# A conditioning vector spread by products with ones, one norm's scaling on another engine, and new planner numbers in a two-network kernel

## The chip, the core and the metric

The kernel runs on one core of a Trainium2 chip. The core has a matrix engine (TensorE, PE in the profile), a vector engine (VectorE, DVE), an activation engine (ScalarE, ACT), a general one (GpSimd, POOL) and a queue engine that issues transfers here (SyncE, SP). The engines run side by side and wait for each other through semaphores. The metric is the device time of one execution in microseconds; a kernel's time is the median of its runs.

## The reference, cut to what matters

512 tokens of width 1024 pass two networks one after the other, in float32. The first has a convolution layer and an attention layer with forget gates, each followed by a gated feed-forward layer and by layer norms; every layer is modulated by a vector that is computed from `c`. The second mixes latent attention and a gated linear attention (HGRN2), followed by a feed-forward layer and a gated projection of `p`.

```python
c_act = jax.nn.silu(c)
for l in range(DEPTH):
    sh1, sc1, g1, sh2, sc2, g2 = jnp.split(c_act @ w_ada[l] + b_ada[l], N_MOD, axis=-1)
    h = modulate(x, sh1, sc1)
    y = short_conv_mixer(...) if l < N_A else forgetting_attention(...)
    x = layer_norm(DEEPNORM_ALPHA * x + g1[:, None, :] * y, ln1_g[l], ln1_b[l])
    h = modulate(x, sh2, sc2)
    y = swiglu(h, ffn_w_gate[l], ffn_w_up[l], ffn_w_down[l])
    x = layer_norm(DEEPNORM_ALPHA * x + g2[:, None, :] * y, ln2_g[l], ln2_b[l])
...
h = rms_norm(x, g_mix)
c_q, c_kv, k_r, hq, hf_f, hf_b, hi, hg = jnp.split(h @ w_in, IN_SPLITS, axis=-1)
x = x + jnp.concatenate([mla(c_q, c_kv, k_r, ...), hgrn2(hq, hf_f, hf_b, hi, hg, ...)], axis=-1) @ w_o
x = x + (silu(rms_norm(x, g_ffn) @ w_gate) * (rms_norm(x, g_ffn) @ w_up)) @ w_down
out = x + sigmoid(rms_norm(x, g_ple) @ w_ple_gate) * (p @ w_ple_proj)
```

## The kernel before

Activations lie transposed: 8 tiles of 128 features by 512 tokens. Each float32 operand of a weight product is split into a high and a low part of a shorter format, and one product is three matmuls: high by high, low by high, high by low. The names say which: `h_0h` and `h_0l` are the parts of the convolution's input tile 0, `whi` and `wlo` those of a pack of eight 128 by 128 weight blocks. A pack arrives as one transfer of 512 KB (`raw`), ACT casts it to `whi`, and DVE, or at some places POOL, subtracts to get `wlo`.

The stages follow the reference. `setup` (L957) loads `vec` (all small vectors), computes `pple` (the projection of `p`, tiles `pT`, which needs nothing else) and spreads `c` over 128 partitions as `cact`; the modulation vectors `ada` are products of rows of `w_ada` with `cact`, summed along the row on DVE. `conv_block` multiplies by three matrices (`gb`, `gc`, `vv`). `fox_block` is the forgetting attention: `pq`, `pk`, `pv` are its projections, `q0a`, `q0b`, `qz` its queries, written on 64 partitions, and `S` its scores. `ffn_ln` with `mix_ln` (L1530) is the second feed-forward layer and the layer norm behind it, done in two halves of 256 tokens; `axr` is the stream, `hx` its scaled split for the next network, and `cq` the first products there. `rope_tables` (L1494) builds sine and cosine from `posi`. In `block2` the latent attention has `MS`, `MP`, `mtp` (scores, probabilities, their transposes), and the tiles `gl`, `gs` belong to the linear attention.

All instructions are first recorded (so nearly all have one line in the profile, L603), then ordered by `plan()` and issued. `plan()` is a list scheduler: it walks in time over the five engines and gives each the ready instruction with the lowest number, by durations from `cost()` (L317) and a table of latencies. The number is the place in the program, less a shift of the instruction's group, a stage or a piece of one: `op.prio = op.i - op.shift - OFFSETS.get(op.group, 0)`. A DVE `tensor_tensor` without PSUM operands may go to POOL when DVE's queue is long; the planner counts that a DVE instruction with two SBUF operands, or a copy or scaling within SBUF, and a POOL `tensor_tensor` do not run side by side. The order inside an engine is then fixed; on the chip an engine waits at an instruction until its operands are there. SP issues all transfers in a fixed order too, on eight semaphores in turn, so each waits for the landing of the eighth before it.

## Time and profile before

| | us |
|---|---|
| median of 3 runs (lowest, highest) | 1895.33 (1893.64, 1896.21) |
| the profiled execution | 1893.86 |
| its span | 1892.2 |
| PE busy | 1868.3 |
| DVE busy | 1216.5 |
| ACT busy | 857.5 |
| POOL busy | 204.7 |
| mean granted clock of PE | 0.998 of full |

The span is the time from the first to the last recorded instruction; the execution's own time has a little around it. PE is almost never idle, so the views that count are those that show where it is, or where it runs slower: the table by windows, the list of what PE waited for, and the timeline around those places. An idle stretch of another engine costs nothing unless PE waits at its end.

### The profile page before, as it was taken

Reading aid. Unit: us, or ns where it says so; the run is one execution under the profiler, and the core shown is the slowest. Engines: PE = TensorE matmul, PEld = TensorE weight load, DVE = VectorE, ACT = ScalarE, POOL = GpSimd, SP = SyncE. Lnnn points to the kernel's source line nnn. Section 1 sums busy time; section 2 is a strip of 40 time slices with the busy share of each in tenths; the row PEclk is TensorE's granted clock in tenths of the full one; section 3 lists DMA queues with packets and bytes.
Section 4 is the critical chain, followed back from the end, with each engine's and each line's share of the span. In section 5 each row is a group of like instructions: output and inputs, shape, how many; then the busy total and the mean of one; then the engine's idle time right before and its main releaser. Section 6 shows DMA issues by size and latency. Waiting matters only on the chain.

```text
span 1892.2 us, 24315 instructions
## 1 busy us (share of the span) xinstructions
PE 1868.3 (99%) x9314; PEld 1572.5 (83%) x9314; DVE 1216.5 (64%) x2000; ACT 857.5 (45%) x1425; POOL 204.7 (11%) x204
## 2 busy tenths in 40 slices
PE   9999999999999999999999999999999999999998
PEld 7888888888888888898888888888887888888887
DVE  8887866567468876885333225998998645344455
ACT  5322722223339876663222223687886423122333
POOL 3101100000010210101000001023343000000000
PEclk9999999999999999999999999999999999999999
DMA  9675377467433113223232222322021322222331
GB/s 353 229 249 190 110 236 239 172 222 243 158 129 108 70 68 122 86 72 106 89 112 100 90 79 105 129 90 79 33 78 45 112 97 92 100 95 95 112 143 69
DMA packets 74325, 241.51 MB, mean 128 GB/s; under 512 B 8320, under 2 KB 9600, under 8 KB 74208
## 3 DMA queue, kind: packets, MB, share of 16 engines
q1 hardware_dynamic: 74208, 239.95, 36.6%
q8 instruction: 73, 1.20, 0.2%
q14 instruction: 44, 0.36, 0.1%
HBM read 231.46 MB, written 8.45 MB: 127 GB/s over the span
## 4 chain that ended last, share of the span: by engine, by line
PE 89%; DVE 6%; ACT 3%; issue 1%; DMA 1%; SPq 0%; DVEq 0%; ACTq 0%
PE pg L603 18%; PE pu L603 18%; PE pd L603 13%; PE gt L603 5%; PE ffn_down L603 5%; PE pv L603 2%; PE gb L603 2%; PE gc L603 2%; PE vv L603 2%; PE pk L603 2%; PE pl L603 2%; PE wo L603 2%; PE pq L603 2%; PE cq L603 2%; PE attn_o L603 1%; PE conv_out L603 1%
## 5 line engine op out<-in xcount | busy, mean ns | idle before, releaser
L603 ACT CAST whi<-raw 128x1024 fp32r<-128x1024 f32 (+1 forms) x313 | 325.4, 1043 | 616.2 <-PE pu L603 126.9
L603 DVE TENSOR_TENSOR wlo<-raw,whi 128x1024 fp32r<-128x1024 f32 (+1 forms) x287 | 354.4, 1238 | 337.0 <-ACT whi L603 321.5
L603 POOL TENSOR_TENSOR wlo<-raw,whi 128x1024 fp32r<-128x1024 f32 x26 | 67.6, 2602 | 1114.9 <-ACT whi L603 952.9
L603 DVE CUSTOM_DVE_ANT_0 aj<-ada,cact,adab 128x1024 bf16<-128x1024 f32 x96 | 126.3, 1318 | 32.5 <-DMA ada<-in_wada 32.0
L603 DVE TENSOR_TENSOR s<-pu,s 128x512 f32<-128x512 f32 x44 | 30.1, 687 | 46.5 <-PE pu L603 46.2
L603 ACT ACTIVATE s<-s 128x512 f32<-128x512 f32 x22 | 13.9, 632 | 77.1 <-DVE s L603 77.1
L603 ACT ACTIVATE s<-pg 128x512 f32<-128x512 f32 x44 | 26.0, 594 | 49.1 <-PE pg L603 49.1
L603 DVE TENSOR_TENSOR s<-pg,rfr 128x512 f32<-128x512 f32 x22 | 15.2, 690 | 40.4 <-PE pg L603 40.2
L603 DVE TENSOR_TENSOR S<-S,sq 128x512 f32<-128x512 f32 (+1 forms) x61 | 34.6, 567 | 0.4
L603 DVE CUSTOM_DVE_ANT_0 G<-S,cmask 128x128 f32<-128x128 f32 (+3 forms) x64 | 28.4, 487 | 4.2 <-PE S L603 3.4
L603 DVE TENSOR_TENSOR u<-pu,rfr 128x512 f32<-128x512 f32 x22 | 15.2, 690 | 23.4 <-PE pu L603 23.4
L603 DVE TENSOR_TENSOR xr<-pd,xr 128x512 f32<-128x512 f32 x16 | 11.0, 689 | 23.0 <-PE pd L603 23.0
L603 ACT ACTIVATE sq<-axr 128x256 f32<-128x256 f32 (+1 forms) x33 | 15.2, 467 | 21.1 <-DVE axr L603 21.1
L603 POOL MEMSET kz<- 32x512 f32 x32 | 16.8, 524 | 50.2 <-PE pd L603 14.7
L603 ACT ACTIVATE Pa<-G,negm 128x128 f32<-128x128 f32 (+1 forms) x32 | 16.2, 508 | 9.8 <-DVE negm L603 4.8
L603 PE MATMUL pg<-hm0l,whi 128*128 128x512 f32 (+1 forms) x48 | 18.0, 376 | 1.2 <-DVE hm0l L603 1.2
L603 PE MATMUL S<-kz,qz 128*128 128x256 f32 (+2 forms) x64 | 19.1, 329 | 0.0
L603 PE MATMUL pg<-hm3l,whi 128*128 128x512 f32 (+1 forms) x48 | 17.9, 373 | 1.0 <-DVE hm3l L603 1.0
L603 PE MATMUL pg<-hm6h,whi 128*128 128x512 f32 (+1 forms) x48 | 17.9, 373 | 0.8 <-ACT whi L603 0.8
L603 PE MATMUL pg<-hm0h,whi 128*128 128x512 f32 (+1 forms) x48 | 18.0, 376 | 0.6 <-ACT hm0h L603 0.6
L603 POOL MEMSET qz<- 32x512 f32 x32 | 17.0, 531 | 14.2 <-DVE ada L603 8.8
L603 PE MATMUL pg<-hm0h,wlo 128*128 128x512 f32 (+1 forms) x48 | 18.0, 374 | 0.5 <-DVE wlo L603 0.5
(3641 smaller groups left out, 6246.1 us busy)
## 6 DMA issues: line engine op xcount, KB each, us to landing
raw<-in_wpack SPq DMA_DIRECT2D x309, 512.0 KB
ada<-in_wada SPq DMA_DIRECT2D x96, 512.0 KB
ada<-in_wada SPq DMA_DIRECT2D x32, 256.0 KB
x<-in_xT SPq DMA_DIRECT2D x8, 256.0 KB
pd<-pple SPq DMA_DIRECT2D x8, 256.0 KB
xd<-x SPq DMA_DIRECT2D x8, 256.0 KB
axr<-xd SPq DMA_DIRECT2D x8, 256.0 KB
xd<-axr SPq DMA_DIRECT2D x8, 256.0 KB
```

Of the source, the lines that this page charges most:

```text
L603: getattr(getattr(nc, op.unit), op.name)(*[get(x) for x in op.args], **{k: get(x) for k, x in op.kw.items()})
```

## The change

Five edits.

- `c` was spread by one transfer (its row read 128 times, 512 KB) followed by one ACT instruction, Silu, on 128 by 1024. Now two transfers bring two rows of 512 elements, two float32 matmuls with a row of ones (`cps`, one row of weights) spread them into PSUM, and two ACT instructions apply Silu from there. The tile `ones` is written first on POOL.
- In `mix_ln` the scaling by the norm's gain and bias, sixteen DVE instructions (two per tile), is now an ACT instruction each.
- `cost()`: outputs with fewer than 128 partitions and 256 or more columns count 115 ns more on ACT, and on DVE in its general case; a small float32 matmul with such an output counts less; `tensor_tensor_reduce` has a smaller fixed part.
- The table of shifts is another one throughout; two of its lines are shown.
- Two small memsets of the mask `gmask` were recorded four times (once per head) and are now recorded once.

```diff
--- before.py
+++ after.py
@@ -88,32 +88,36 @@
 FREE_LAT = {"g": 220, "s": 220, "o": 220, "whi": 200, "wlo": 200}
 
 OFFSETS = {
-    "attn_o_2": 460, "attn_o_ln0": 40, "attn_o_ln1": -100, "attn_o_st1": 1590, "conv0": 2530, "conv1": 3820,
...
+    "attn_o_1": 1300, "attn_o_3": -20, "attn_o_ln0": 40, "attn_o_ln1": -200, "attn_o_st1": 7330,
...
 }
@@ -331,25 +335,26 @@
             if n == "transpose":
                 return 109
             if dt == F32:
-                return 4 + max(4 * size / 2.4, 193)
+                return 4 + max(4 * size / 2.4, 193 if outs[0].shape[0] == P else 113)
             return 13.4 + max(size / 2.4, 95) if dt == F32R else 3 + size / 2.4
         psum = any(x.tile.cls in PSUM_CLS for x in ins)
         cols = sum(1 for x in ins if isinstance(x, View) and x.idx.size == 1)
+        part = 115 if outs[0].shape[0] < P and size >= 256 else 0
         if op.eng == "ACT":
-            return (51 if psum else 94) + 0.8333 * size + 93 * (cols + ("accum_out" in op.kw))
+            return (51 if psum else 94) + 0.8333 * size + 93 * (cols + ("accum_out" in op.kw)) + part
         if op.eng == "POOL":
             return 200 + 2.13 * size if n == "tensor_tensor" else 36 + 0.8333 * size
         if n in ("tensor_tensor_reduce", "tensor_reduce"):
             size = int(ins[0].idx.size)
         if n == "tensor_tensor_reduce":
-            return 112 + 1.0417 * size + 61 * cols
+            return 77 + 1.0417 * size + 61 * cols
         if n in ("tensor_scalar", "tensor_copy", "memset") and not psum:
             return 68 + 0.5208 * size + 61 * cols
         if n == "tensor_tensor_scan":
             return 68 + 2.0833 * size
         if n == "reciprocal":
             return 68 + 6.4 * size
-        return 68 + 1.0417 * size + (61 * cols if size > 1 else 0)
+        return 68 + 1.0417 * size + (61 * cols if size > 1 else 0) + part
 
 
 class Engine:
@@ -958,18 +963,28 @@
         nc, a = self.nc, self.a
         self.vec = self.c("vec", (P, NVEC))
         cact = self.c("cact", (P, D))
+        self.ones = self.c("ones", (P, P))
+        nc.gpsimd.memset(self.ones, 1.0)
         nc.fifo = True
         self.warm_up()
         self.ple_inputs()
         self.ple_projection(0)
         nc.shift = 1000
-        nc.sync.dma_start(cact, a["c"].to_broadcast((P, D)))
+        row = [self.f(f"c{i}", (1, T)) for i in range(2)]
+        for i in range(2):
+            nc.sync.dma_start(row[i], a["c"][:, i * T:(i + 1) * T])
         first = VC["conv_w"]
         nc.sync.dma_start(self.vec[:, :first], a["vec"][:, :first])
         nc.shift = 0
         self.ple_projection(1)
         nc.group = ""
-        self.act(cact, cact, AF.Silu)
+
+        for i in range(2):
+            ps = self.ps("o", f"cps{i}")
+            nc.shift = 1000
+            nc.tensor.matmul(ps, self.ones[:1], row[i], start=True, stop=True)
+            self.act(cact[:, i * T:(i + 1) * T], ps, AF.Silu)
+            nc.shift = 0
         self.cact = cact
         self.ada = self.c("ada", (P, 112))
         self.adab = self.c("adab", (P, 112))
@@ -986,8 +1001,6 @@
         nc.gpsimd.memset(self.ident, 1.0)
         nc.gpsimd.affine_select(self.ident, self.ident, [[-1, P]], ALU.is_equal, 0.0,
                                 base=0, channel_multiplier=1)
-        self.ones = self.c("ones", (P, P))
-        nc.gpsimd.memset(self.ones, 1.0)
         self.onesr = self.c("onesr", (P, P), F32R)
         nc.vector.tensor_copy(self.onesr, self.ones)
         self.onesd = self.c("onesd", (P, P))
@@ -1540,7 +1553,7 @@
                 d = self.ax[f]
                 nc.vector.tensor_tensor(d[:, sl], d[:, sl], st["mu", p], ALU.subtract)
                 nc.vector.tensor_tensor(d[:, sl], d[:, sl], r, ALU.mult)
-                self.scaled(d, g[:, f:f + 1], b[:, f:f + 1], sl)
+                nc.scalar.activation(d[:, sl], d[:, sl], AF.Identity, bias=b[:, f:f + 1], scale=g[:, f:f + 1])
                 if p == 0:
                     acts.append((f, self.r(f"hx{f}h"), self.r(f"hx{f}l")))
                 self.scale_split(d, self.v("g_mix", f), acts[f][1:], sl)
@@ -1767,9 +1780,6 @@
         scale = float(192 ** -0.5)
         mx = self.small(f"mx{h}", 4)
         rs = self.small(f"mrs{h}", 4)
-
-        nc.gpsimd.memset(self.gmask[:64, 0, 64:], 1)
-        nc.gpsimd.memset(self.gmask[64:, 1, :64], 1)
         Ps = []
         for i in range(4):
             tb = slice(i * P, (i + 1) * P)
@@ -1812,6 +1822,9 @@
             t = self.f(f"at{d}", (P, 4, P))
             nc.gpsimd.memset(t, 0.0)
             self.at.append(t)
+
+        nc.gpsimd.memset(self.gmask[:64, 0, 64:], 1)
+        nc.gpsimd.memset(self.gmask[64:, 1, :64], 1)
 
     def sigmoid(self, z, name):
```

How the rows move is shown at three places. First PE at the start: `pple` as above, with `pT0h`, `pT0l`, `pT1h` the parts of `p`; before:

```order
L603 MATMUL pple_192<-pT0l,whi_152 128x512
L603 MATMUL pple_192<-pT0h,wlo_160 128x512
L603 MATMUL pple_157<-pT1h,whi_152 128x512
L603 MATMUL pple_157<-pT1l,whi_152 128x512
L603 MATMUL pple_157<-pT1h,wlo_160 128x512
```

and now:

```order
L608 MATMUL pple_193<-pT0l,whi_153 128x512
L608 MATMUL pple_193<-pT0h,wlo_161 128x512
L608 MATMUL cps_199<-c_95,ones 128x512
L608 MATMUL cps_209<-c_98,ones 128x512
L608 MATMUL pple_158<-pT1h,whi_153 128x512
L608 MATMUL pple_158<-pT1l,whi_153 128x512
```

The two `cps` products stand between the products with `pT0` and those with `pT1`. ACT there, from the cast of the second pack to the first convolution tile, before:

```order
L603 CAST whi_196<-raw_90 128x1024
L603 COPY pple_202<-pple_157 128x512
L603 ACTIVATE cact<-cact 128x1024
L606 ACT_TABLE_LOAD
L603 CAST whi_242<-raw_101 128x1024
L603 COPY pple_256<-pple_162 128x512
L603 COPY pple_265<-pple_174 128x512
L603 COPY pple_270<-pple_192 128x512
L603 COPY pple_291<-pple_232 128x512
L603 COPY pple_300<-pple_240 128x512
L603 COPY pple_310<-pple_251 128x512
L603 ACTIVATE h_0h<-x_118,ada 128x512
```

and now:

```order
L608 CAST whi_197<-raw_91 128x1024
L608 ACTIVATE cact<-cps_199 128x512
L608 ACTIVATE cact<-cps_209 128x512
L611 ACT_TABLE_LOAD
L608 CAST whi_248<-raw_105 128x1024
L608 COPY pple_259<-pple_158 128x512
L608 COPY pple_265<-pple_163 128x512
L608 COPY pple_272<-pple_175 128x512
L608 COPY pple_276<-pple_193 128x512
L608 CAST whi_298<-raw_178 128x1024
L608 ACTIVATE h_0h<-x_120,ada 128x512
L608 ACTIVATE x_120<-x_120 128x512
```

Three copies of `pple` tiles have moved behind `h_0h`, the two Silu instructions stand at the place of the one, and another cast stands ahead of `h_0h`. PE's first convolution products now have the last five `pple` products between them:

```order
L608 MATMUL pple_278<-pT1h,whi_197 128x512
L608 MATMUL gc_316<-h_0h,whi_248 128x512
L608 MATMUL vv_318<-h_0h,whi_248 128x512
L608 MATMUL gb_322<-h_0h,whi_248 128x512
L608 MATMUL gc_325<-h_0h,whi_248 128x512
L608 MATMUL pple_278<-pT1l,whi_197 128x512
L608 MATMUL vv_342<-h_0h,whi_248 128x512
L608 MATMUL pple_278<-pT1h,wlo_214 128x512
L608 MATMUL gb_346<-h_0h,whi_248 128x512
L608 MATMUL pple_289<-pT1h,whi_197 128x512
L608 MATMUL pple_289<-pT1l,whi_197 128x512
L608 MATMUL pple_289<-pT1h,wlo_214 128x512
```

Second, PE at the attention's first scores, before (`pk` and `pq` are independent products; `q0a` comes from `pq_5208`, whose last product stands 45 rows above `S`):

```order
L603 MATMUL pk_5329<-hk5h,whi_5166 128x512
L603 MATMUL pk_5329<-hk5l,whi_5166 128x512
L603 MATMUL pk_5329<-hk5h,wlo_5185 128x512
L603 MATMUL pk_5329<-hk6h,whi_5166 128x512
L603 MATMUL pk_5329<-hk6l,whi_5166 128x512
L603 MATMUL S_0_5400<-k0a,q0a 128x256
L603 MATMUL S_1_5404<-k0a,q0a 128x256
```

and now (`q0a` comes from `pq_5216`, whose last product stands 20 rows above `S`):

```order
L608 MATMUL pq_5413<-hq1l,whi_5277 128x512
L608 MATMUL pq_5413<-hq1h,wlo_5287 128x512
L608 MATMUL pq_5413<-hq2h,whi_5277 128x512
L608 MATMUL pq_5413<-hq2l,whi_5277 128x512
L608 MATMUL pq_5413<-hq2h,wlo_5287 128x512
L608 MATMUL S_0_5435<-k0a,q0a 128x256
L608 MATMUL S_0_5435<-kz_207,qz_348 128x256
```

The first `S` was row 3007 of PE and is row 3022; what stands just ahead of it is another query projection. Third, the norm of `mix_ln`, ACT's rows around the first `hx0h`, before:

```order
L603 CAST whi_10543<-raw_10484 128x1024
L603 ACTIVATE sq_10443<-axr_7262 128x256
L603 ACTIVATE ffn_down1musq_10552<-ffn_down1st_10536 128x256
L603 COPY ffn_down1mu_10554<-ffn_down1st_10536 128x256
L603 ACTIVATE hx0h<-axr_7233,vec 128x256
L603 ACTIVATE S_10563<-axr_7233 128x256
L603 ACTIVATE hx1h<-axr_7236,vec 128x256
```

and now:

```order
L608 CAST whi_10549<-raw_10490 128x1024
L608 ACTIVATE axr_6821<-axr_6821,vec 128x256
L608 ACTIVATE sq_10449<-axr_6842 128x256
L608 ACTIVATE hx0h<-axr_6821,vec 128x256
L608 ACTIVATE S_10562<-axr_6821 128x256
L608 ACTIVATE axr_6824<-axr_6824,vec 128x256
L608 ACTIVATE ffn_down1musq_10580<-ffn_down1st_10520 128x256
L608 COPY ffn_down1mu_10584<-ffn_down1st_10520 128x256
L608 ACTIVATE hx1h<-axr_6824,vec 128x256
```

and DVE's rows that lead there, before:

```order
L603 TENSOR_TENSOR axr_7233<-axr_7233,ffn_down1rstd 128x256
L603 TENSOR_TENSOR axr_7236<-axr_7236,ffn_down1rstd 128x256
L603 TENSOR_TENSOR wlo_10549<-raw_10484,whi_10543 128x1024
L603 TENSOR_SCALAR axr_7233<-axr_7233,vec 128x256
L603 TENSOR_SCALAR axr_7236<-axr_7236,vec 128x256
```

and now:

```order
L608 TENSOR_TENSOR axr_6821<-axr_6821,ffn_down1rstd 128x256
L608 SCALAR_TENSOR_TENSOR axr_6842<-ffn_down17B,ada,axr_6842 128x256
L608 TENSOR_TENSOR axr_6827<-axr_6827,ffn_down1rstd 128x256
L608 TENSOR_TENSOR wlo_10556<-raw_10490,whi_10549 128x1024
L608 SCALAR_TENSOR_TENSOR hx0l<-axr_6821,vec,hx0h 128x256
```

The scalings have gone from DVE's rows to ACT's, and ACT reads the first of them before the second half's statistics. PE has two of the statistics products (`ffn_down1st` with `S`) fourteen rows further up, between the last `ffn_down17B` products. On DVE the instructions on the position table stand three rows later than before, behind more of the feed-forward layer's, with two `wlo` between them. In POOL's row there are 31 `wlo`, where there were 26.

## Rows read from the trace of the kernel before

**Rows 1.** The page, part 1: busy us, share of the span, instructions.
```profile
PE 1868.3 (99%) x9314; PEld 1572.5 (83%) x9314; DVE 1216.5 (64%) x2000; ACT 857.5 (45%) x1425; POOL 204.7 (11%) x204
```

**Rows 2.** Table by windows: start:end, length, busy us by engine, clock, DMA share, GB/s.
```profile
0.00:50.00 50.00, 46.50 (x208) 37.58 (x209) 40.71 (x97) 28.82 (x39) 14.90 (x37) 0.97 0.97 355
...
600.00:650.00 50.00, 48.76 (x292) 42.48 (x291) 41.85 (x108) 42.45 (x105) 10.11 (x10) 1.00 0.27 95
...
1150.00:1200.00 50.00, 47.65 (x298) 43.05 (x297) 39.79 (x75) 22.68 (x44) 5.83 (x5) 0.97 0.27 95
...
1400.00:1450.00 50.00, 46.24 (x284) 38.10 (x285) 46.65 (x77) 35.70 (x67) 27.59 (x22) 1.00 0.17 65
```

**Rows 3.** Timeline of PE at the start: start us, us, instruction, idle before and releaser.
```profile
8.18 0.39 PE L603 MATMUL pple<-pT1h,whi 128*128 128x512 f32 x1
...
12.48 0.39 PE L603 MATMUL pple<-pT0h,whi 128*128 128x512 f32 x1
...
17.04 0.39 PE L603 MATMUL pple<-pT1h,wlo 128*128 128x512 f32 x1
19.32 0.50 PE L603 MATMUL gc<-h_0h,whi 128*128 128x512 f32 x1 [1.90 <-ACT h_0h L603]
...
20.38 0.63 PE L603 MATMUL gc<-h_0h,whi 128*128 128x512 f32 x1
...
23.76 0.39 PE L603 MATMUL vv<-h_0h,whi 128*128 128x512 f32 x1
```

**Rows 4.** Timeline of ACT at the start.
```profile
9.78 1.05 ACT L603 CAST whi<-raw 128x1024 fp32r<-128x1024 f32 x1 [2.01 <-DMA raw<-in_wpack]
...
11.58 1.06 ACT L603 ACTIVATE cact<-cact 128x1024 f32<-128x1024 f32 x1 [0.27 <-DMA cact<-in_c]
...
18.45 0.81 ACT L603 ACTIVATE h_0h<-x,ada 128x512 fp32r<-128x512 f32 x1 [0.53 <-DVE ada L603]
```

**Rows 5.** One tile, `krop`: count, duration ns min/median/max, first and last start us.
```profile
L603 PE MATMUL krop<-krg,perm x2: 590/590/591, 1251.8 to 1252.2; 128*128 128x512 f32 x2
```

**Rows 6.** Timeline of all engines at the first `S` of the attention.
```profile
609.35 0.58 ACT L603 ACTIVATE qz<-pq 64x512 fp32r<-64x512 f32 x1
...
611.08 0.58 ACT L603 ACTIVATE q0b<-pq 64x512 fp32r<-64x512 f32 x1
...
611.69 0.68 DVE L603 SCALAR_TENSOR_TENSOR q0a<-pq,q0a 64x512 fp32r<-64x512 f32 x1 [0.75 <-ACT q0b L603]
...
612.43 0.68 PE L603 MATMUL S<-k0a,q0a 128*128 128x256 f32 x3 [1.08 <-DVE q0a L603]
```

**Rows 7.** Timeline of DVE, and of PE, around the position table.
```profile
875.65 0.43 DVE L603 CAST posf<-posi 128x512 f32<-128x512 int32 x1 [6.76 <-DMA posi<-in_pos]
...
891.74 0.50 PE L603 MATMUL pg<-hm0h,wlo 128*128 128x512 f32 x1 [0.47 <-DVE wlo L603]
```

**Rows 8.** Timeline of all engines at the norm before the second network.
```profile
1186.16 1.10 DVE L603 TENSOR_TENSOR axr<-axr,ffn_down1rstd 128x256 f32<-128x256 f32 x2
...
1188.33 0.72 DVE L603 TENSOR_SCALAR axr<-axr,vec 128x256 f32<-128x256 f32 x2
1188.76 0.51 ACT L603 ACTIVATE hx0h<-axr,vec 128x256 fp32r<-128x256 f32 x1 [0.64 <-DVE axr L603]
...
1189.32 0.74 PE L603 MATMUL cq<-hx0h,whi 128*128 128x256 f32 x4 [1.88 <-ACT hx0h L603]
...
1191.07 0.42 PE L603 MATMUL cq<-hx0h,wlo 128*128 128x256 f32 x1
...
1191.50 0.41 PE L603 MATMUL cq<-hx0h,wlo 128*128 128x256 f32 x1
```

**Rows 9.** Tiles `MP`, `Pb` (as in rows 5); list of PE's waits: us, times, longest.
```profile
L603 DVE TENSOR_SCALAR MP<-MP,mrs x16: 468/479/2578, 1294.5 to 1436.9; 128x512 f32<-128x512 f32 x16
...
L603 DVE TENSOR_SCALAR Pb<-Pb,rs x16: 477/479/482, 623.5 to 781.4; 128x512 f32<-128x512 f32 x16
...
PE mtp L603 <- DVE MP L603: 1.7, 1, 1.7
```

54 rows, old and new, of the table OFFSETS are left out of this document.

## Prediction

> **What bounds the kernel now.** I read the shares of busy time first. PE is busy in 1868.3 of 1892.2 us, and no other engine passes 64% [rows 1]. So the span is PE's list of matmuls plus what PE loses, and what it loses is small: idle time of 1892.2 - 1868.3 = 23.9 us, and stretches in which it runs at a lower clock. A product of 512 columns costs 0.228 us while the clock is full: the starts at 12.48 and 17.04 us are 20 products apart [rows 3]. No edit here removes a weight product, so the change can only win or lose in the gaps. The reader should therefore look for the stretches in which PE's busy time falls below the window's length, and then for what PE waits for there.
>
> The table by windows gives the stretches [rows 2]: the first 50 us (3.5 us idle, granted clock 0.97), the forgetting attention at 600 to 650 (1.2 idle), the norm before the second network at 1150 to 1200 (2.35 idle, clock again 0.97), and the linear attention at 1400 to 1450 (3.8 idle). The list of waits puts one name on each: the first product of the convolution waits 1.9 us for `h_0h`, `cq` waits 1.9 for `hx0h`, `mtp` 1.7 for `MP`, and `S` 1.1 for `q0a` [rows 6, 7, 8, 9].
>
> At the start, PE finishes the last `pple` product that begins at 17.04 and begins `gc` at 19.32; the gap is followed by slow products (0.63 us long at 20.38 instead of 0.39), and product number 13 of this stage begins at 23.76 [rows 3]. Projected back at 0.228 us each, 12 products, the stage began at 23.76 - 2.7 = 21.0. So the wait and the low clock behind it together put PE some 21.0 - 17.3 = 3.7 us behind. The records show one of the two levels, 1.2 GHz instead of 2.4, between about 20 and 23 us, after an idle stretch of 1.90 us. The norm at 1189 shows the same pair: 1.88 us idle before `cq`, then 256-column products 0.215 us apart (1191.07 and 1191.50 are two apart) where half of 0.228, 0.114, belongs to the full clock [rows 8].
>
> **The change, part by part.**
>
> *Conditioning vector.* Removed: a DMA of 512 KB and one ACT instruction of 1.06 us. Added: two DMAs of 2 KB, two fp32 products of 512 columns with one row, two ACT instructions of 512 columns. On ACT the nearest row for a 512-column activation is `h_0h` at 0.81 us with two column operands; two of these are at most 1.6 us against 1.06, so 0 to 0.6 us more on ACT [rows 4]. On PE an fp32 product of 512 columns leaves two records of 590 ns, 0.4 us apart [rows 5]; I take 0.85 us for each, 1.7 for the two (that row has 128 rows of weights, the new one a single row; less is possible, and I keep 0.9 to 1.7). On the DMA queue the cast that waits for the pack ahead ends its wait at 9.78 and the one that waits for the broadcast at 11.58 [rows 4]: the broadcast holds the stream for 1.8 us, and everything behind it comes up to that much earlier. At 355 GB/s [rows 2] 512 KB are 1.5 us. I take 1.5.
>
> What of this is on the path? The two new products stand in PE's row in front of a product that began at 8.18 [rows 3]. The rows of `c` are issued behind the pack that landed at 9.7, so PE waits there for them, up to 1.5 us, if they land in turn; if small transfers pass the pack, PE does not wait at all. The two products and this wait take the place of idle time that PE had later: 8.2 + 1.5 + 1.7 = 11.4, then 31 `pple` products to 18.4, then the first `gc`, with the other five `pple` products filled in among the first conv products. `h_0h` must be there at 18.4: it ended at 19.26, behind a DVE product that waited for the conditioning weights, and these now arrive 1.5 us earlier, so I put it at 17.8 to 18.5. With the five moved products, 1.1 us, the stage begins in effect at 19.5 instead of 21.0: a gain of 1.5 us. Bounds: if the earlier idle time of 1.5 us brings the low clock itself, its cost (21.0 - 19.3 = 1.7 us) comes back and the gain is -0.2; if `c` lands early and the stream is 1.8 us ahead, it is 2.5.
>
> The Trainium skill speaks against small transfers: "DMA: Bandwidth & Descriptors", section "Rules for kernel authors", says that many small transfers should be joined into one large one, since below 64 KB mostly overhead is paid. No row here shows a 2 KB transfer landing in a loaded queue. By that rule taken at its strongest the two rows would hold the queue about as long as the broadcast did, nothing would be won at the start, and the sum below would be 2.6 instead of 4.1.
>
> *One norm's scaling on ACT.* Sixteen DVE instructions of 0.36 us each leave DVE, sixteen come to ACT; the nearest ACT row, `hx0h`, of the same size, takes 0.51 [rows 8]. In the first half, `hx0h` now follows on ACT directly after the scaling, and DVE's row has no 1.2 us `wlo` between the normalised tile and its scaling any more. In the trace that scaling began at 1188.33 and `hx0h` at 1188.76, ending 1189.27, and PE went on at 1189.32. The tile was normalised near 1186.7 (the first of two in 1.10 us from 1186.16). Without the detour the scaling can begin there on ACT; then come a square and `hx0h`, three times 0.51, so 1188.2. PE has moved two of its statistics products ahead and comes 0 to 0.5 us earlier. Of the 1.88 us some 1.1 go, and the low clock behind it perhaps as well (at the start it cost 1.7). Against it stands that ACT now has a scaling, a `hx` and a square per tile, at most 1.5 us, where PE needs 12 x 0.114 = 1.4 us, with four more ACT instructions of the second half's statistics between them: ACT has no slack there. I take 0.8; bounds 0 and 1.1 + 1.7 = 2.8.
>
> *Durations for 64 partitions, and the new shifts.* These cost nothing by themselves; they change the order. At the first `S` of the attention PE waited 1.08 us for a chain on ACT and DVE of 609.35 to 612.37: four ACT instructions on 64 partitions and one on DVE [rows 6]. The planner had counted these 64-partition instructions shorter. Now the first `S` stands 15 rows later in PE's list, with independent products ahead of it. Those 15 rows are 3.4 us, but the products that `q0a` reads end later too: 19 products, 4.3 us, lie between them and `S`, where the chain needs 3.1 us and one cast (1.0) may stand before it. Just enough: I take 1.2 of the 1.4 us (1.08 and some 0.3 to restart), bounds -0.5 and 1.4.
>
> At 891.74 PE waited 0.47 for a `wlo` on DVE, which had stood behind the position table: DVE was held 6.76 us by that table's DMA [rows 7]. In the new order the table's instructions stand behind more of the hidden-layer work and `wlo` stands between them. I take 0.6 (the wait and the restart), bounds 0 and 0.6.
>
> In the linear attention nothing in the lists says which way it goes: the same pieces stand there in another order, and 3.8 us of idle time can shrink or grow. I take 0, bounds -2 and +2. At the three norms inside the first network PE's list is row for row the same: 0. The mask's memsets on POOL and the two planner constants else: 0, since POOL is busy for 11% [rows 1].
>
> One more effect is moved work: the list has 31 `wlo` on POOL instead of 26. The Trainium skill, "SBUF — State Buffer", section "SBUF: two separate sides", says that DVE and GpSimd share a pair of ports as an exclusive lock, and whoever comes second waits for the whole instruction. The rows bear it out in one place and not in another: the scaling of `MP` takes 479 ns in the median and once 2578, beside a `wlo` on POOL, while the sixteen scalings of `Pb` in the attention, a stretch with `wlo` on POOL as well, lie between 477 and 482 [rows 9]. By the rule the sum loses 1.7 for each `wlo` that meets such a scaling.
>
> By rows alone: a held instruction costs 2578 - 479 = 2.1 us, and PE lost 1.7 behind it once; I take 0 for the five, and make the other a rival.
>
> *Sum.* 1.5 + 0.8 + 1.2 + 0.6 = 4.1 us. The profiled execution took 1893.86 (span 1892.2 and 1.7 around it), so its counterpart is 1889.8. The median before is 1895.33, 1.5 above the profiled one; against it the forecast is 1891.2. The measurement can tell about 0.2%, 3.8 us, from no change: faster means below 1891.5, slower above 1899.1. My point is just on the faster side.
>
> **The rivals.**
>
> *The gain at the start is given back* (the same). The two new products make PE wait at 8.2 us, the clock falls there, and `h_0h` is no earlier, since DVE and ACT set it and not the stream. For it: an idle time of about this length was twice followed by the low clock. Against: PE idled 1.08 us at 612 without a lower clock [rows 2, 6]. Then -0.2 stands in place of 1.5, and with the attention's chain just missing (0 for 1.2) the sum is 1.2: 1894.1.
>
> *Slower: `wlo` on POOL holds DVE where PE waits.* In place: attention and linear attention, where the five new ones stand beside scalings of `Pa`, `Pb` and `MP`. Price: 1.7 us of PE for each that hits. It decides from the fifth hit: 5 x 1.7 = 8.5 turns -4.1 into +4.4, 1899.7. For it: the one long `MP` row; against it: the 16 undisturbed `Pb`, and that the planner already counts the lock.
>
> *The new order also empties the linear attention.* If the waits of `mtp` and its neighbours go (3.8 us at 1400 to 1450, of which some 3.5 can go), and the norm gives its 2.8: 4.1 + 3.5 + 2.0 = 9.6, so 1885.7.
>
> *It does not do what it says.* The waits that the trace names are set by arrivals that the planner does not see, and move on with the order: 0 +- 1.5, 1895.
>
> **How the numbers follow.** Forecast 0.40 (1889 to 1893, just over half of it faster); gain lost at the start 0.18; emptied linear attention 0.25; nothing 0.08; slower 0.09. Faster: 0.24 + 0.25 + a little of the others = 0.50; slower 0.09 and the far end of "nothing" = 0.11; within 0.2%: 0.39. The range reaches from 1885.5, the emptied case, to 1896.5, which holds the two cases without gain and leaves out the slower one.
>
> **What would show it.** Right: `cps` products at 8 to 11.5 us, no wait before `gc` above 0.5 us, no 0.63 us products in the first 25 us, and the window 0 to 50 with a clock of 1.00. The wait of `cq` under 0.8 us and no half clock at 1190; no wait of `S` for `q0a`; none of `pg` for `wlo` near 890. Wrong: half clock at 9 to 13 us; `h_0h` at 19 or later; `cq` or `pu` products waiting one after another for `hx` tiles (ACT bound); any DVE scaling of about 2.5 us beside a POOL `wlo` with PE idle behind it.

## The result and the profile after

| | before | changed |
|---|---|---|
| median, us (lowest, highest, runs) | 1894.49 (1891.66, 1896.21, 4) | 1883.95 (1883.70, 1885.88, 4) |
| the profiled execution's span, us | 1892.2 | 1882.2 |
| PE busy, us | 1868.3 | 1864.1 |
| DVE, ACT, POOL busy, us | 1216.5, 857.5, 204.7 | 1202.7, 865.5, 216.0 |

The ratio is 0.9948, interval 0.9931 to 0.9965: the changed kernel is 0.5% faster, about 10 us, where 4.1 were forecast; it lies outside the range, on its lower side. The profiled execution of one kernel below, `after_old_mix`, ran with a mean granted clock of 0.65 and took 2656 us; it is left out, and that kernel has a time from its other five and no row in the table of stages. The page of the changed kernel, part 1, against [rows 1]:

```profile
PE 1864.1 (99%) x9318; PEld 1573.4 (84%) x9318; DVE 1202.7 (64%) x1978; ACT 865.5 (46%) x1442; POOL 216.0 (11%) x204
```

The table by windows for the stretches of [rows 2] (columns as there):

```profile
0.00:50.00 50.00, 48.28 (x221) 38.79 (x222) 42.58 (x91) 30.40 (x42) 14.79 (x37) 1.00 0.95 343
600.00:650.00 50.00, 49.90 (x299) 43.92 (x298) 39.48 (x104) 40.96 (x96) 15.84 (x13) 1.00 0.27 94
...
1150.00:1200.00 50.00, 47.79 (x337) 44.25 (x336) 37.72 (x82) 30.04 (x67) 3.57 (x4) 1.00 0.27 96
1400.00:1450.00 50.00, 48.48 (x266) 40.46 (x265) 44.03 (x72) 34.41 (x64) 15.95 (x14) 0.97 0.24 85
```

The first 50 us have 1.72 us of idle time instead of 3.50 and a full clock, 600 to 650 has 0.10 instead of 1.24. The norm before the second network still has 2.21 (2.35 before), but no low clock. The linear attention at 1400 has 1.52 instead of 3.76, now with a clock of 0.97.

PE's timeline at the start, against [rows 3]:

```profile
8.33 1.98 PE L608 MATMUL cps<-c,ones 1*128 1x512 f32 x4
...
18.22 0.50 PE L608 MATMUL gc<-h_0h,whi 128*128 128x512 f32 x1 [0.67 <-ACT h_0h L608]
...
19.02 0.39 PE L608 MATMUL gc<-h_0h,whi 128*128 128x512 f32 x1
...
23.90 0.39 PE L608 MATMUL gc<-h_0l,whi 128*128 128x512 f32 x1
```

The four `cps` records are the two fp32 products; from the first of them to the next `pple` product at 10.24 it is 1.91 us. PE does not wait for `c`. `gc` begins at 18.22 after 0.67 us of idle time, and the products behind it are 0.39 to 0.40 long: the clock stayed up.

At the first `S` of the attention, all engines, against [rows 6]; the first row is the kernel before's, of the product just ahead of its `S` (612.43):

```profile
610.96 0.39 PE L603 MATMUL pk<-hk6l,whi 128*128 128x512 f32 x1
```

```profile
608.69 2.40 POOL L608 TENSOR_TENSOR wlo<-raw,whi 128x1024 fp32r<-128x1024 f32 x1 [43.26 <-ACT whi L608]
...
610.66 0.68 DVE L608 SCALAR_TENSOR_TENSOR q0a<-pq,q0a 64x512 fp32r<-64x512 f32 x1 [1.45 <-ACT q0b L608]
...
611.85 0.39 PE L608 MATMUL pq<-hq2h,wlo 128*128 128x512 f32 x1
612.08 0.28 PE L608 MATMUL S<-k0a,q0a 128*128 128x256 f32 x1
```

`q0a` on DVE is ready at 611.34, `S` begins at 612.08 and waits for nothing; a `wlo` runs on POOL ahead of it. From the start of the product ahead to the start of `S` it was 1.47 us and is 0.23: 1.24 us less. At the norm, all engines, against [rows 8]:

```profile
1176.27 1.02 PE L608 MATMUL ffn_down1st<-S,onesd 128*128 128x256 f32 x4
...
1180.24 0.70 PE L608 MATMUL ffn_down1st<-axr,onesd 128*128 128x256 f32 x2 [1.29 <-DVE axr L608]
...
1180.68 0.49 ACT L608 ACTIVATE hx0h<-axr,vec 128x256 fp32r<-128x256 f32 x1
...
1181.22 0.77 PE L608 MATMUL cq<-hx0h,whi 128*128 128x256 f32 x4
...
1184.30 0.39 PE L608 MATMUL cq<-hx1l,whi 128*128 128x256 f32 x1 [0.38 <-DVE hx1l L608]
```

`cq` no longer waits for `hx0h`. But PE waits 1.29 us one step earlier, for `axr` on DVE (0.37 before), and then a little for single low parts `hx1l`, `hx3l`. The four `ffn_down1st<-S` records at 1176.27 stood behind the last `ffn_down17B` product before; now it begins at 1178.67. The wait at 891.74 of [rows 7] is gone. The head of the list of PE's waits, against the last row of [rows 9], shows what is left:

```profile
PE gs00A L608 <- DVE gl00x L608: 1.4, 1, 1.4
PE ffn_down1st L608 <- DVE axr L608: 1.3, 1, 1.3
...
PE mtp L608 <- DVE MP L608: 1.1, 1, 1.1
...
PE cq L608 <- DVE hx1l L608: 0.4, 1, 0.4
```

**Where the 10 us came from.** The starts of five products mark the stages: the first `conv_out5A` ends the start and the convolution, `ffn_down07A` the first feed-forward layer, `attn_o5A` the attention, `ffn_down17A` the second feed-forward layer but its end, the last `ffn_down17B` the first half of the norm, and the last product of all the second network. The table has, for each profile, how much shorter (-) or longer (+) each stage is than in the kernel before, in us; its rows below the first are the experiments.

| profile | start, conv. | ffn 0 | attention | ffn 1 | its end | second network | all |
|---|---|---|---|---|---|---|---|
| changed | -2.0 | 0.0 | -4.2 | -0.7 | +0.9 | -3.9 | -10.0 |
| c_only | -1.5 | 0.0 | 0.0 | -1.0 | 0.0 | +1.8 | -0.7 |
| costs_only | -0.6 | 0.0 | +1.1 | +0.1 | 0.0 | +8.9 | +9.4 |
| table_only | -0.7 | 0.0 | +3.3 | -0.6 | +0.8 | +12.0 | +15.0 |
| mix_only | -0.1 | 0.0 | -0.1 | -0.6 | 0.0 | +1.2 | +0.3 |
| after_old_table | -1.8 | 0.0 | +1.1 | -1.1 | 0.0 | +0.7 | -1.2 |
| after_old_cost | -2.2 | +1.1 | +3.1 | -0.3 | +0.8 | +8.4 | +11.0 |
| after_old_c | -0.4 | +0.2 | -4.2 | -0.7 | +0.9 | -5.0 | -9.2 |
| c_same_order | -1.5 | 0.0 | -4.1 | -0.7 | +0.9 | -5.1 | -10.5 |
| mix_same_order | -1.4 | +1.3 | -4.2 | -0.7 | +0.9 | +0.2 | -3.9 |
| wlo_same_order | -1.4 | 0.0 | +1.1 | -0.6 | +0.9 | -6.6 | -6.7 |
| att_old_shifts | -1.0 | +0.1 | +1.2 | -0.4 | +0.9 | -4.9 | -4.2 |
| net2_wlo_dve | -2.1 | 0.0 | -4.2 | -0.6 | +0.9 | -6.6 | -12.7 |
| net2_old_shifts | -1.6 | +0.1 | -4.2 | -0.6 | +0.8 | -1.5 | -7.0 |
| after_beside | -2.8 | 0.0 | -4.1 | -0.7 | +0.8 | -3.8 | -10.4 |
| net2_beside | -1.0 | 0.0 | -4.2 | -0.7 | +0.9 | -6.3 | -11.2 |

The +0.9 of "its end" is no loss: it is the four statistics records that moved ahead of the last `ffn_down17B`, and the second network has them no longer. The attention and the second network brought 8 of the 10 us; the forecast had put 1.2 and 0.8 there.

### The profile page after: what moved, and what is told of

Its sections match the earlier page's. It is cut to its first block, busy times and chain, and to the rows that moved or that the text cites. A ratio compares the mean times of both kernels' runs of the same rounds, so it can differ in the third digit from the quotient of the medians.

```text
span 1882.2 us, 24358 instructions
## 1 busy us (share of the span) xinstructions
PE 1864.1 (99%) x9318; PEld 1573.4 (84%) x9318; DVE 1202.7 (64%) x1978; ACT 865.5 (46%) x1442; POOL 216.0 (11%) x204
## 5 line engine op out<-in xcount | busy, mean ns | idle before, releaser
L608 DVE TENSOR_TENSOR wlo<-raw,whi 128x1024 fp32r<-128x1024 f32 (+1 forms) x282 | 344.7, 1225 | 338.0 <-ACT whi L608 328.8
L608 POOL TENSOR_TENSOR wlo<-raw,whi 128x1024 fp32r<-128x1024 f32 x31 | 76.2, 2461 | 907.1 <-ACT whi L608 633.1
L608 ACT ACTIVATE sq<-x 128x256 f32<-128x256 f32 (+1 forms) x19 | 9.8, 516 | 18.9 <-DVE x L608 18.6
L608 PE MATMUL pg<-hm0h,whi 128*128 128x512 f32 (+1 forms) x48 | 17.8, 376 | 0.6 <-ACT hm0h L608 0.6
L608 PE MATMUL pu<-hm0h,wlo 128*128 128x512 f32 (+1 forms) x48 | 18.0, 376 | 0.0
```

The source lines that it names most:

```text
L608: getattr(getattr(nc, op.unit), op.name)(*[get(x) for x in op.args], **{k: get(x) for k, x in op.kw.items()})
```

## The experiments

Two ways of undoing something were used. In the first eight, and in the two with old shifts (`att_old_shifts`, `net2_old_shifts`), the code, the durations or the table were changed and the planner made a new plan. In the others every engine's order is that of the changed kernel, and single instructions are exchanged behind the planner; then no row moves but what is named. The change of the mask's memsets was not tried alone.

### One part of the change alone

**The conditioning vector alone** (`c_only`): the kernel before with the hunk of `setup`:

```diff
-        nc.sync.dma_start(cact, a["c"].to_broadcast((P, D)))
+        for i in range(2):
+            nc.sync.dma_start(row[i], a["c"][:, i * T:(i + 1) * T])
...
-        self.act(cact, cact, AF.Silu)
+            nc.tensor.matmul(ps, self.ones[:1], row[i], start=True, stop=True)
+            self.act(cact[:, i * T:(i + 1) * T], ps, AF.Silu)
```

> The kernel before with the first edit alone (two rows, two products with ones); table and durations as before. Theory of sites (each edit pays at its own place): the stage of the convolution's products ends 1.5 to 2.0 us earlier and everything behind it keeps that, 1892.5 to 1893.5 against 1894.5; no low clock in the first 25 us. Rival (the gain comes from the new table of shifts, which was found for this code): under the old table h_0h is ordered as before, the start gives 0.5 or less and later stages wander by 1 to 2 us either way.

Measured: 1891.38 against 1893.18, ratio 0.9990 (0.9981 to 0.9999). By the medians 1.8 us, as the theory of sites said. In the profile, of the slowest of the ten executions, the start gains 1.5, and 1.8 are lost in the second network, though nearly all rows there, and the list of PE's waits, are those of the kernel before: the low clock follows the wait of `mtp` here (at 1435), and that of `cq` there (at 1191).

**The durations alone** (`costs_only`): the kernel before with the hunk of `cost()`, as

```diff
+        part = 115 if outs[0].shape[0] < P and size >= 256 else 0
...
-            return (51 if psum else 94) + 0.8333 * size + 93 * (cols + ("accum_out" in op.kw))
+            return (51 if psum else 94) + 0.8333 * size + 93 * (cols + ("accum_out" in op.kw)) + part
```

> The kernel before with the corrected durations alone; table as before. Theory of durations: the attention (pq to attn_o) gains most of the 4.2 us that it gained, 3 or more, and no other stage moves by more than 1: 1891 to 1892. Rival (the table): the attention gains 0 to 1.5 (only the wait of S for q0a), the rest wanders by up to 2 us: 1893 to 1896.

Measured: 1902.26 against 1893.18, ratio 1.0045 (1.0029 to 1.0062). Both expectations fall: the attention is 1.1 longer, not shorter, and the second network is 8.9 longer. Its window shows where that goes: 8.66 us of idle time, and low clock as well.

```profile
1250.00:1450.00 200.00, 191.34 (x998) 158.20 (x998) 186.41 (x300) 153.01 (x275) 81.22 (x68) 0.97 0.19 66
```

**The table alone** (`table_only`): the kernel before with the new `OFFSETS`.

```diff
-    "attn_o_2": 460, "attn_o_ln0": 40, "attn_o_ln1": -100, "attn_o_st1": 1590, "conv0": 2530, "conv1": 3820,
...
+    "attn_o_1": 1300, "attn_o_3": -20, "attn_o_ln0": 40, "attn_o_ln1": -200, "attn_o_st1": 7330,
```

> The kernel before with the new table of shifts alone; durations and code as before. Theory of the table: the attention gains 3 or more, the position table's wait goes (0.6), the linear attention gains 1 to 2: 1889 to 1891, the start and the norm as before. Rival (durations and sites): shifts found for other durations do not fit, every stage behind the start is between 1 us better and 2 us worse: 1893 to 1898.

Measured: 1909.25, ratio 1.0085 (1.0070 to 1.0100): 16 us slower, more than either expected. 12.0 of them are lost in the second network and 3.3 in the attention, where twelve `wlo` stand on POOL, as in the changed kernel (seven in the kernel before). PE's list of waits in the attention has

```profile
PE pq L607 <- ACT hq5h L607: 0.9, 1, 0.9
PE po L607 <- DVE PT_0l L607: 0.9, 2, 0.7
```

**The scaling on ACT alone** (`mix_only`): the kernel before with

```diff
-                self.scaled(d, g[:, f:f + 1], b[:, f:f + 1], sl)
+                nc.scalar.activation(d[:, sl], d[:, sl], AF.Identity, bias=b[:, f:f + 1], scale=g[:, f:f + 1])
```

> The kernel before with the norm's scaling on ACT alone. Theory of sites: up to the norm nothing changes (within 0.3 us), the wait of cq falls from 1.9 to below 0.8 and the low clock behind it goes, the norm's stretch gains 1 to 2 us: 1892.5 to 1893.5. Rival (ACT becomes the bound there): waits of cq for one hx tile after the other, and the norm's stretch gains under 0.5.

Measured: 1893.32, ratio 1.0000 (0.9991 to 1.0009). No gain; the second network is 1.2 longer in the profile.

So none of these four parts is worth the gain, two are harmful alone, and the sum of the four is +24 us by the profiles where the whole is -10.

### One part undone

**The old table** (`after_old_table`): the changed kernel with the old `OFFSETS`, the hunk above reversed.

> The changed kernel with the old table of shifts. Theory of the table: the gain of the attention (4.2) and of the linear attention (1.5) is lost or most of it, only the start's and the norm's remain: 1889 to 1892. Rival (durations and sites): the attention keeps 3 or more, at most 2 us are lost in all: 1884 to 1887.

Measured: 1893.13 against 1893.24, ratio 0.9999 (0.9990 to 1.0009). The theory of the table holds, and more: by the medians all the other edits together give nothing without it.

**The old durations** (`after_old_cost`): the hunk of `cost()` reversed.

> The changed kernel with the old durations. Theory of durations: the attention loses 3 us or more of its 4.2 and the wait of S for q0a is back: 1887 to 1889. Theory of the table: the attention loses 1.5 or less: 1884 to 1886.

Measured: 1903.70, ratio 1.0056 (1.0041 to 1.0071). The attention loses 7.3 us and the second network 12.3. The four corners for the attention are: old durations and old table 0; new durations +1.1; new table +3.3; both -4.2. Twelve `wlo` stand on POOL in the attention here too (3.1 us longer than before), so their number alone does not bring its gain. The shifts belong to the durations with which they were found.

**The old spreading of `c`** (`after_old_c`): the hunk of `setup` reversed.

> The changed kernel with the old spreading of c (one transfer of 512 KB). Theory of sites: the convolution's products end 1.5 to 2.0 us later, the wait of gc for h_0h is near 1.9 us again with low clock behind it, and the later stages keep their gains: 1885.5 to 1886.5. Rival: the start loses 0.5 or less, since the new order at the start brings the gain.

Measured: 1884.39, ratio 0.9953 (0.9938 to 0.9968), beside 0.9948 for the changed kernel: nothing that the intervals can tell. The profile has the 1.6 us at the start that were expected, with low clock; but 1.1 of them are regained in the second network, where the order is the same as in the changed kernel. What differs there is the clock (below).

**The scaling on DVE again** (`after_old_mix`): the hunk of `mix_ln` reversed.

> The changed kernel with the norm's scaling on DVE again. Theory of sites: the same up to the norm, then the wait of cq and the low clock are back and 1 to 2 us are lost there: 1885 to 1886. Rival: the norm loses under 0.5, and what moves is the linear attention behind it.

Measured: 1900.37 against 1893.24, ratio 1.0040 (1.0026 to 1.0054). Some 17 us lost by sixteen small instructions: either they matter that much, or the new plan does; the next group tells.

### The order kept, single instructions exchanged

**The old transfer in the new order** (`c_same_order`):

```diff
+        if op.name == "dma_start" and name(op.args[0]) == "c0":
+            op.args = (cact, aps["c"].to_broadcast((P, D)))
+        elif op.name == "dma_start" and name(op.args[0]) == "c1":
+            continue
+        elif op.name == "matmul" and name(op.args[0]).startswith("cps"):
+            continue
```

> The changed kernel with every engine's order as it is, and in the place of the first row of c the old transfer of 512 KB into cact (no products with ones, Silu from SBUF). Theory (the transfer itself is what the start pays): the convolution's products end 1.5 to 2.0 us later than in the changed kernel, gc waits near 1.9 us for h_0h again and a stretch of low clock follows it, and the later stages keep their gains: 1885.5 to 1886. Rival (the order pays, not the transfer): 0.5 or less is lost.

Measured: 1885.32, ratio 0.9956 (0.9941 to 0.9971). In the profile the convolution ends 1.5 us before that of the kernel before, without the new rows. The eight profiles with the new start in its own order fall into two kinds: in three (the changed kernel, `after_beside`, `net2_wlo_dve`) the rows are there when PE comes to `cps`, the clock stays up and the gain is 2.0 to 2.8; in the other five PE waits 0.5 to 1.1 us for them at 8.3, low clock follows (a granted clock of 0.89 over the first 15 us), and the gain is 1.0 to 1.6. So in this profile the order alone brings 1.5, and the new transfer 0.5 to 1.3 more where its rows land in time and nothing where they do not. That is no division of the gain: the profile is of the fastest of four executions (1883.26; the others 1884.42, 1886.22 and 1886.87, with mean granted clocks of 0.999, 0.998 and 0.998 where this one had 1.000), its clock stayed up after 2.13 us of idle time, and by the medians the old transfer is 1.4 slower than the changed kernel, with intervals that overlap. Two profiles with the old order and the old transfer had no low clock there either, and gain 0.1 (`mix_only`) and 0.6 (`costs_only`). So both the order and the transfer seem to pay, and how much each does stays open. In PE's timeline `h_0h` begins on ACT at 17.7 instead of 17.4, and the two products only fill the wait.

```profile
18.56 0.51 PE L608 MATMUL gc<-h_0h,whi 128*128 128x512 f32 x1 [2.13 <-ACT h_0h L608]
...
19.38 0.40 PE L608 MATMUL gc<-h_0h,whi 128*128 128x512 f32 x1
```

Why `h_0h` hardly moves is seen on DVE and ACT, in the changed kernel and then with the old transfer:

```profile
11.68 0.75 DVE L608 CUSTOM_DVE_ANT_0 ada<-ada,cact,adab 128x512 f32<-128x512 f32 x1 [0.32 <-DMA ada<-in_wada]
...
16.40 1.05 ACT L608 CAST whi<-raw 128x1024 fp32r<-128x1024 f32 x1 [1.01 <-DMA raw<-in_wpack]
```

```profile
12.98 0.75 DVE L608 CUSTOM_DVE_ANT_0 ada<-ada,cact,adab 128x512 f32<-128x512 f32 x1 [0.76 <-DMA ada<-in_wada]
...
16.75 1.05 ACT L608 CAST whi<-raw 128x1024 fp32r<-128x1024 f32 x1 [0.89 <-DMA raw<-in_wpack]
```

The old transfer does hold the stream: the first `ada` instruction begins 1.3 us later with it, and over all the profiles at 13.0 to 14.3 with the transfer of 512 KB and at 11.3 to 12.1 with the two rows. But `h_0h` no longer follows `ada`: in the new order the cast of another pack stands ahead of it on ACT, and that cast waits for its own transfer until 16.40 or 16.75.

**The scalings on DVE in the new order** (`mix_same_order`):

```diff
+            op.unit, op.eng, op.name = "vector", "DVE", "tensor_scalar"
+            op.args = (d, d, op.kw["scale"], op.kw["bias"], ALU.mult, ALU.add)
```

> The changed kernel with every engine's order as it is, the norm's sixteen scalings done by DVE at the same places. Theory (after_old_mix lost 17 us by its new plan and not by the engine): up to the norm the same, then the norm's stretch loses 0 to 2 us: 1884 to 1886. Rival (DVE is too full there): 5 us or more are lost in the norm and the second network.

Measured: 1888.14, ratio 0.9974 (0.9965 to 0.9984). The norm and the second network lose 4.1 us of their 3.9, between the two expectations. PE waits for low parts on DVE, one after the other:

```profile
PE gt L608 <- ACT whi L608: 1.3, 1, 1.3
...
PE cq L608 <- DVE hx1l L608: 1.2, 1, 1.2
PE cq L608 <- DVE hx5l L608: 1.1, 1, 1.1
...
PE cq L608 <- DVE hx3l L608: 0.7, 1, 0.7
```

In this order the scaling on ACT is worth 4 to 5 us (5.3 beside `c_same_order`, which has no low clock in the second network either), in the old order (`mix_only`) nothing. A further 1.3 us went in the first feed-forward layer, which this edit doesn't touch: PE waits 1.0 us, until 459.06, for a `wlo` that stands on DVE behind an `ada` instruction, and that one waited for its transfer until 456.57 (454.44 in the changed kernel).

**All `wlo` back on DVE in the new order** (`wlo_same_order`): the 31 subtractions on POOL.

```diff
+        if op.unit == "gpsimd" and op.name == "tensor_tensor" and op.args[0].tile.cls == "wlo":
+            op.unit, op.eng = "vector", "DVE"
```

> The changed kernel with every engine's order as it is, all 31 subtractions wlo that stand on POOL done by DVE at their places. Theory (the places on POOL relieve DVE where PE waits for it): the attention, where twelve of them stand, loses 2 us or more, and the linear attention some: 1887 or more. Rival (a wlo on POOL holds DVE, as the long MP row suggests): the attention loses nothing and long scalings go: 1882 to 1884.

Measured: 1886.89, ratio 0.9966 (0.9953 to 0.9979). Both theories are right, at different places. The attention becomes 5.3 us longer than in the changed kernel; the second network becomes 2.7 us shorter. Three windows over the attention, of the kernel before, the changed one and this one:

```profile
593.00:798.00 205.00, 203.16 (x1182) 175.87 (x1182) 160.35 (x400) 151.98 (x356) 26.55 (x21) 1.00 0.26 93
```

```profile
591.00:792.00 201.00, 200.90 (x1183) 177.33 (x1183) 152.86 (x394) 152.72 (x356) 39.01 (x26) 1.00 0.27 93
```

```profile
592.00:798.00 206.00, 201.91 (x1181) 176.93 (x1181) 164.00 (x404) 152.68 (x355) 9.98 (x14) 1.00 0.27 93
```

POOL has 26.55, 39.01 and 9.98 us of work there (7, 12 and no `wlo`), PE idles 1.84, 0.10 and 4.09 us. This takes all twelve from POOL, so it does not tell what the five additional ones are worth. PE's waits in this kernel's attention are all for DVE:

```profile
PE S L608 <- DVE PT_0l L608: 1.1, 1, 1.1
PE pv L608 <- DVE negm L608: 0.9, 1, 0.9
PE po L608 <- DVE PT_2l L608: 0.6, 1, 0.6
```

**Old shifts for the attention alone** (`att_old_shifts`): the changed kernel, its table with the old entries of the groups `fox`, `rest`, `logf`, `kv`, `v`, `q`, `sc`, `val`, as

```diff
-    "fox": 2200,
+    "fox": 1570,
```

> The changed kernel with the old shifts for the attention's groups alone (from the modulation rest to val); everything else new. Theory (a stage's shifts act in that stage): the attention loses its 4.2 us and about 1 more, as with the whole old table, the second network keeps its 3.9: 1888 to 1890. Rival (a change in one stage scrambles the later ones): the second network moves by more than 3 us too.

Measured: 1889.55, ratio 0.9980 (0.9971 to 0.9990). The theory holds: 5.4 us lost in the attention, 9 `wlo` on POOL there instead of 12, and the second network, with the rows of the changed kernel, keeps its gain. A stage's shifts act in that stage.

**Old shifts for the second network alone** (`net2_old_shifts`): likewise the groups from `lat` to `value` and `w_o2`, as

```diff
-    "state0": 5500,
+    "state0": 730,
```

> The changed kernel with the old shifts for the groups of the second network's mixing alone (lat to value, w_o2). Theory (a stage's shifts act in that stage): the same up to the norm, the second network loses 3 to 5 us of its 3.9: 1887 to 1889. Rival (the scaling on ACT and the durations bring it): it loses 1.5 or less.

Measured: 1886.39, ratio 0.9964 (0.9951 to 0.9977). 2.4 us are lost there, less than expected; beside the profiles of the changed order whose clock stayed up there (-4.9 to -5.1), as it did in this one, it is 3.4 to 3.5. PE waits for ACT instead:

```profile
PE MS L607 <- ACT krs3h L607: 1.3, 1, 1.3
...
PE wo L607 <- ACT mo L607: 1.1, 1, 1.1
PE mpo L607 <- ACT gsq L607: 1.0, 1, 1.0
```

**Only the second network's `wlo` on DVE** (`net2_wlo_dve`, and `net2_beside` beside a second run of the changed kernel, `after_beside`): the exchange of `wlo_same_order`, in this part of the order only:

```diff
+    for op in order[at[0]:end]:     # first cq to last mtp: six of the 31
+        if op.unit == "gpsimd" and op.name == "tensor_tensor" and op.args[0].tile.cls == "wlo":
+            op.unit, op.eng = "vector", "DVE"
```

> The changed kernel with every engine's order as it is; of the 31 subtractions wlo on POOL only the six between the first cq and the last mtp are done by DVE at their places. Theory (in the second network a wlo on POOL holds DVE where PE waits for it, in the attention it relieves DVE): the attention keeps its 4.2 us, the second network gains the 2.7 us that it gained when all 31 moved: 1881 to 1882, faster than both kernels. Rival (those 2.7 were not the second network's own): within 1 us of the changed kernel, 1883 to 1885.

> The changed kernel once more, on the same chip as the next one. The start varies from profile to profile (the convolution's products ended between 1.0 and 2.0 us before those of the kernel before); everything behind it is expected as in the first profile within 0.5 us: 1883 to 1885.

> The version with the six wlo of the second network on DVE, beside the changed kernel on the same chip. Theory (a wlo on POOL holds DVE there): 2 to 2.7 us below after_beside, 1881 to 1882. Rival (the first comparison was between two chips): within 1 us of it.

Measured: 1881.98, ratio 0.9940 (0.9927 to 0.9952); on one chip 1880.89 (1880.69 to 1882.39, ratio 0.9935, 0.9922 to 0.9947) beside 1884.05 (1883.04 to 1884.41, ratio 0.9949, 0.9935 to 0.9962) for the changed kernel. The ranges of the two don't touch: this version is 3 us faster than the changed one and 12.5 faster than the kernel before. The collision is easy to read. In the changed kernel DVE scales the four `MP` while POOL has a `wlo` and then another subtraction, `gr2xl`; DVE's rows, POOL's, and PE's behind them:

```profile
1423.82 4.79 DVE L608 TENSOR_SCALAR MP<-MP,mrs 128x512 f32<-128x512 f32 x4
```

```profile
1423.31 2.82 POOL L608 TENSOR_TENSOR wlo<-raw,whi 128x1024 fp32r<-128x1024 f32 x1 [1.51 <-PE wo L608]
...
1426.09 1.44 POOL L608 TENSOR_TENSOR gr2xl<-gsq,gr2xh 128x512 fp32r<-128x512 f32 x1
```

```profile
1427.87 1.56 PE L608 MATMUL mtp<-ident,MP 128*128 128x128 f32 x7 [1.07 <-DVE MP L608]
...
1430.26 0.63 PE L608 MATMUL wo<-mx4h,wlo 128*128 128x512 f32 x1
```

With the `wlo` on DVE, behind the scalings:

```profile
1424.35 1.66 DVE L608 TENSOR_SCALAR MP<-MP,mrs 128x512 f32<-128x512 f32 x4
1425.93 1.21 DVE L608 TENSOR_TENSOR wlo<-raw,whi 128x1024 fp32r<-128x1024 f32 x1
```

The four scalings take 1.66 us instead of 4.79, and the longest of all sixteen falls from 2596 to 951 ns (tile `MP`, changed kernel and this one):

```profile
L608 DVE TENSOR_SCALAR MP<-MP,mrs x16: 473/478/2596, 1278.4 to 1428.1; 128x512 f32<-128x512 f32 x16
...
L608 DVE TENSOR_SCALAR MP<-MP,mrs x16: 472/476/951, 1278.0 to 1425.5; 128x512 f32<-128x512 f32 x16
```

The wait of `mtp` is gone, and with it, here, the stretch of low clock that followed (0.63 us for a 512-column product at 1430.26). Of the 2.7 us in the table 1.1 are that clock: in three profiles with the `wlo` on POOL and the same rows it stayed up (-4.9 to -5.1). The collision itself is then some 1.6.

## Why the prediction was wrong

The direction was right, and so were the sizes of the start and of the norm. The sum was 4.1 where 10 came because two terms were mis-sized: the attention, where only one wait was counted (1.2 for 4.2), and what lies behind the norm, which was put at nothing (0 for 1.9). Some of the reasons were wrong too.

- **The start** (1.5 forecast, 2.0 measured, 1.7 in the mean of eight profiles): right in size, wrong in its path. The step "the broadcast holds the stream for 1.8 us" held: the first `ada` begins 1.3 us later with it in the same order. What failed is the next step, that `h_0h` stands behind the DVE product that waits for the conditioning weights and so comes earlier by as much: in the new order it stands behind the cast of another pack, and with the broadcast back it is only 0.3 later than in the changed kernel. Part of the gain is the new order, which was not taken apart, part the clock, and part the transfer where its rows land in time. The forecast of `h_0h` (17.8 to 18.5; it ended at 18.17) held; the two `cps` products took 1.91 us, a little over their bound of 1.7.
- **The attention** (1.2 forecast, 4.2 measured): the term that failed most. I took the one wait that the list names and left the rest of the stage at nothing. At that wait the forecast was right: the step to the first `S` fell by 1.24 us. The other 3.0 came from the rest of the stage. A matmul's record is 0.39 us long and the next begins 0.228 later, so the first 0.16 us of each delay are not idle time: the window's idle time fell by 1.74 us only, and the starts, which show the rest, by 4.2. "I take 0 for the five" was not right either: the stage has twelve `wlo` on POOL where it had seven, and with none there it loses 5.3 us (`wlo_same_order`). They are needed in this order but do not bring the gain alone, since the same twelve with the old durations make the stage 3.1 to 3.3 longer. That neither the table nor the durations bring it alone was not in the prediction at all; what in the new order shortened the other delays was not taken apart.
- **The position table** (0.6): 0.7 measured for the stage, the wait gone. That is luck: in `c_only` and `mix_only`, whose rows in this stage are those of the kernel before, the wait of `pg` for `wlo` is gone too and the stage is 1.0 and 0.6 shorter. The table's transfer landed earlier there (DVE waited 5.6 us for it, not 6.8).
- **The norm** (0.8): from the last `ffn_down17B` (1184.77, now 1178.67) to the first `cq` (1189.32, now 1181.22) it was 4.55 us and is 2.55; 0.9 of the 2.0 is the statistics records that moved ahead, so some 1.1 remain, which is what the prediction expected to go. Its bound of 1.7 more for the low clock was wrong: from the first `cq` to the first product with `hx7l` it is 12.15 us with low clock (before) and 12.04 without (`c_only`, the same rows), since `hx7l` is ready 11.98 and 11.99 us after the first `cq` in the two; low clock cost next to nothing there. The step "ACT has no slack there" was wrong in this order: `cq` waits for no tile on ACT, only 0.4 us or less for low parts on DVE, and putting the scalings back on DVE costs 4.1.
- **Behind the norm** (0, bounds -2 and +2 for the linear attention): of the second network's -3.9 the moved records and the norm leave 1.9. The wait of `mtp` fell from 1.7 to 1.1, and low clock followed it in this profile, which costs 1.1; its own shifts are worth 2.4 (`net2_old_shifts`). A wait in the feed-forward layer is gone that the prediction didn't name, in the kernel before:

```profile
1495.05 0.50 PE L603 MATMUL pu<-hf4h,whi 128*128 128x512 f32 x1 [0.89 <-ACT whi L603]
```

- **The rivals.** "The new order also empties the linear attention" (0.25, 1885.7) was the nearest in number, by luck: it priced 3.5 for the linear attention and 2.0 more for the norm, where all behind the norm gave 1.9 and the norm its 1.1, and it left the attention at 1.2. "`wlo` on POOL holds DVE where PE waits" was right as a mechanism in the second network, some 1.6 us and the clock behind it, but the kernel before already paid it, and there are 6 `wlo` on POOL between the first `cq` and the last `mtp` where there were 7, so it could not make the change slower. The sixteen undisturbed `Pb` that were held against it say nothing: in the kernel before no subtraction on POOL ran beside any of them. "The gain at the start is given back" came true in its mechanism in five of the eight profiles with the new start: PE waits for `c` and the clock falls. But 1.0 to 1.6 us of the gain are left there, where -0.2 was priced, for `h_0h` begins at 16.7 to 17.5 there instead of 18.45.

## What to carry to other kernels

A table of priorities that was searched for one program and one set of durations is part of that program: taken apart, the two lost 9 to 16 us against the kernel before, and together with the code they gained 10, so such a change is to be judged as a whole, from the waits that remain in its order, and not as a sum of its edits. Moving work to GpSimd paid here where VectorE was what PE waited for, in an order that was planned with it, and cost where scalings from SBUF stood next to it; look for one instruction that takes five times its median, and when it finds none, whether the two ran side by side at all. To size what a stage can still give, take the spacing of PE's starts, not its idle time. And before the cost of low clock is counted as a gain, look whether what PE needs next is there by then: at the norm it was not.

## What was not expected of the hardware

- How long PE idled doesn't tell whether low clock follows. In the start of `c_same_order` it idled 2.13 us and the next products were 0.40 long (rows above); in `mix_same_order` it idled 0.72 at 8.37 and they were 0.63 long, as in all five profiles with a wait there:

```profile
8.37 1.95 PE L608 MATMUL cps<-c,ones 1*128 1x512 f32 x4 [0.72 <-DMA c<-in_c]
...
11.43 0.63 PE L608 MATMUL pple<-pT1h,whi 128*128 128x512 f32 x1
```

  In [rows 3] low clock followed 1.90 us of idle time; in `mix_only` it did not follow 1.61 us at the same place. Behind the wait of `mtp`, the two profiles of the changed kernel have low clock, and `c_same_order`, `after_old_c` and `att_old_shifts`, with the same wait of 1.1 us and the same rows, have not: that is the 1.1 us by which their second network is shorter. What decides was not found.
- With the same instructions in the same order, the two rows of `c` land before PE asks for them in three profiles and 0.5 to 1.1 us after in five.
- A DVE scaling of 478 ns took 2596 beside a `wlo` on POOL, the next 1479 beside `gr2xl`, and the group of four 4.79 us instead of 1.66 (rows of `MP` above); the `wlo` took 2.82 us. The Trainium skill ("SBUF — State Buffer", "SBUF: two separate sides") says that the two engines share a pair of ports, which DVE uses for some kinds of instruction, and that the one that starts first keeps it for its whole instruction while the other stands still; the trace agrees, with 2596 ns, that a scaling can wait out most of a `wlo`.
